# Attention over short sequences: the division of the outputs moves from VectorE to GpSimd, and the loads are issued five chunks ahead

## The chip, the cores and the metric

The kernel runs on one core of a Trainium2 chip. The metric is the device time of one execution in microseconds (us). Three runs of the kernel before took 143.09 us in the median (142.85 to 143.81). The profile is that of one further execution.

The core has five engines that run side by side and wait for one another through semaphores: TensorE (matmul, "PE" in the profile, its weight loads "PEld"), VectorE ("DVE"), ScalarE ("ACT"), GpSimd ("POOL") and SyncE ("SP"). Each works through its own list of instructions in order. Data come from HBM to SBUF and go back through 16 DMA engines. Matmuls write into PSUM, which has eight banks of 2 KB per partition. GpSimd issues the loads here, and SyncE the stores.

## The reference

```python
# q, k, v: (32, 12, 128, 64) float32: batch, heads, sequence, head dimension
scale = 1.0 / np.sqrt(64)
scores = scale * np.matmul(q, k.transpose(0, 1, 3, 2))
scores_max = np.max(scores, axis=-1, keepdims=True)
attn = np.exp(scores - scores_max)
attn = attn / (np.sum(attn, axis=-1, keepdims=True) + 1e-8)
return np.matmul(attn, v)
```

There are 384 heads of 128 x 64. Each input and the output hold 12.6 MB. The kernel leaves out the maximum (the inputs are small), and divides at the end: it multiplies the unnormalized outputs by the reciprocals of the row sums.

## The kernel before

The 384 heads are cut into NCH = 24 chunks of 16 heads. A chunk's q, k and v are three loads of 128 partitions x 1024 elements, which the DMA casts from float32 to bfloat16 on the way. Each partition holds runs of consecutive rows of one head (16 rows of q and k, 4 rows of v).

What happens to chunk c:

- `turn(c, 0)` and `turn(c, 1)`: VectorE transposes q and k in 32 x 32 blocks, SBUF to SBUF (tiles qt and kt), so that the head dimension comes to lie on the partitions.
- `scores(c)`: 32 small matmuls write all 16 score blocks to s_ps, which fills four PSUM banks and has one buffer; ScalarE takes the exponential of all 2048 columns in one instruction (attn).
- `values(c, part)`: two halves of v go through matmuls with a permuted identity (perm) into v_ps, one bank, and ScalarE copies them to v2 in SBUF.
- `denominators(c)`: four matmuls with a matrix of ones give the row sums (d_ps).
- `outputs(c, j)`: 16 matmuls for each half j of the head dimension give the transposed outputs (o_ps). d_ps and o_ps share a ring named w_ps.
- `divide(c, d_ps)`: VectorE turns the sums into SBUF (dt) and takes their reciprocals (recip, 16 per partition).
- `finish(c, j, o_ps)`: VectorE turns half j of the outputs, and multiplies it by the reciprocals into o_sb.
- `store(c)`: SyncE issues one DMA of 512 KB from o_sb.

The order of the instructions on each engine is the order of the Python code: everything stands under a manual schedule, and nothing reorders it. The body of the loop over c works on several chunks at once: scores of c+1, values of c+2, the turns of c+2, and denominators, outputs and store of c. On TensorE the order within one pass is scores(c+1), first half of values(c+2), denominators(c), outputs(c, 0), second half of values(c+2), outputs(c, 1).

Waits come from data and from buffers. A pool with `bufs` = n lets the writer of a tile wait for the readers of the tile n before it. Ahead of the loop GpSimd issues all 72 loads one behind the other. The input tiles of all 24 chunks have buffers of their own, so no load waits for a buffer; each load waits for the completion of the load eight places before it, whose semaphore it takes over. The stores wait for one another in the same way, eight places back.

PSUM's eight banks: s_ps four, v_ps one, w_ps two, ot_ps one. The last of these holds the turned outputs between the two steps of `finish`.

Of the kernel before, what the change touches and what calls it, by code (L numbers as in the profile page):

```python
# [9 lines left out]
@with_exitstack  # L10
def kernel(
    ctx: ExitStack,
    tc: tile.TileContext,
    q: bass.AP,
    k: bass.AP,
    v: bass.AP,
    out: bass.AP,
):

    nc = tc.nc
    f32 = mybir.dt.float32
    bf16 = mybir.dt.bfloat16

    B, H, S, D = q.shape
    assert S == 128 and D == 64
    scale = 1.0 / (D ** 0.5)
    TQ = 16  # L30
    GQ = S // TQ
    T = 4
    A = 4
    G = S // T
    CB = 4
    NCH = B * H // (A * CB)

    def runs(x, t):
        return x.rearrange("b h (g t) d -> (b h g) (t d)", t=t).rearrange(
            "(n p) x -> p n x", p=128)  # L40

    qr, kr, vr, orr = runs(q, TQ), runs(k, TQ), runs(v, T), runs(out, TQ)

    singles = ctx.enter_context(tc.tile_pool(name="singles", bufs=1))
    pin = ctx.enter_context(tc.tile_pool(name="pin", bufs=NCH))
    pt = ctx.enter_context(tc.tile_pool(name="pt", bufs=3))
    pa = ctx.enter_context(tc.tile_pool(name="pa", bufs=3))
    pf = ctx.enter_context(tc.tile_pool(name="pf", bufs=2))
    po = ctx.enter_context(tc.tile_pool(name="po", bufs=3))
    ps = ctx.enter_context(tc.tile_pool(name="ps", bufs=1, space=bass.MemoryType.PSUM))  # L50

    chunks, qts, attns, v2s, osbs = {}, {}, {}, {}, {}

    def load_qk(c):
        for src, which in ((qr, 0), (kr, 1)):
            x = pin.tile([128, TQ, D], bf16, tag="qk"[which] + "_bf", name="qk"[which] + "_bf")
            nc.gpsimd.dma_start(out=x, in_=src[:, c, :].rearrange("p (t d) -> p t d", t=TQ))  # L57
            chunks[c, which] = x

    def load_v(c):  # L60
        x = pin.tile([128, CB, T, D], bf16, tag="v_bf", name="v_bf")
        nc.gpsimd.dma_start(  # L62
            out=x, in_=vr[:, c * CB:(c + 1) * CB, :].rearrange("p n (t d) -> p n t d", t=T))
        chunks[c, 2] = x

    with tc.manual_schedule():
        load_qk(0)
        ident = singles.tile([128, 128], bf16)
        make_identity(nc, ident)
        perm = singles.tile([128, A, 4, GQ], bf16)  # L70
        nc.vector.tensor_copy(  # L71
            perm.rearrange("p a th g -> p a g th"),
            ident.rearrange("p (a g th) -> p a g th", a=A, th=4))
        ones = singles.tile([128, 32], bf16)
        nc.vector.memset(ones, 1.0)

        load_v(0)
        for c in range(1, NCH):
            if c < NCH - 1:
                load_v(c)  # L80
            load_qk(c)
        load_v(NCH - 1)

        def turn(c, which):


            x = chunks.pop((c, which)).bitcast(f32)
            xt = pt.tile([128, 4, S], f32, tag="qk"[which] + "t", name="qk"[which] + "t")
            if which == 0:
                nc.vector.transpose(xt.rearrange("p h (x g) -> p x h g", g=GQ), x)  # L90
            else:
                nc.vector.transpose(xt.rearrange("p h (x g) -> p x h g", g=GQ),  # L92
                                    x.rearrange("p (th tp) e -> p tp th e", tp=4))
            qts[c, which] = xt.bitcast(bf16).rearrange("p h (s j) -> p h s j", j=2)

        def scores(c):
            qt, kt = qts.pop((c, 0)), qts.pop((c, 1))
            s_ps = ps.tile([128, 4, 4, S], f32, tag="s_ps", name="s_ps")
            for h in range(4):
                for j in range(2):  # L100
                    for b in range(4):
                        pr = slice(b * 32, (b + 1) * 32)
                        nc.tensor.matmul(  # L103
                            s_ps[:, b, h, :], lhsT=kt[pr, h, :, j], rhs=qt[pr, h, :, j],
                            start=(j == 0), stop=(j == 1), tile_position=(b * 32, 0))
            attn = pa.tile([128, 4, 4, S], bf16, tag="attn", name="attn")
            nc.scalar.activation(out=attn, in_=s_ps, func=mybir.ActivationFunctionType.Exp,  # L107
                                 bias=0.0, scale=scale)
            attns[c] = attn

        def values(c, part):

            v_bf = chunks[c, 2]
            if part == 0:
                v2s[c] = pa.tile([128, A, CB, D], bf16, tag="v2", name="v2")
            v_ps = ps.tile([128, 2, CB, D], f32, tag="v_ps", name="v_ps")
            for i in range(2):
                for t in range(T):
                    nc.tensor.matmul(  # L119
                        v_ps[t * G:(t + 1) * G, i],  # L120
                        lhsT=perm[:, 2 * part + i].rearrange("p th g -> p (th g)"),
                        rhs=v_bf[:, :, t, :], start=True, stop=True, tile_position=(0, t * G))
            nc.scalar.copy(v2s[c][:, 2 * part:2 * part + 2], v_ps)  # L123

        def denominators(c):

            d_ps = ps.tile([128, 4, S], f32, tag="w_ps", bufs=2, name="d_ps")
            for b in range(4):
                nc.tensor.matmul(  # L129
                    d_ps[b * 32:(b + 1) * 32], lhsT=ones, rhs=attns[c][:, b],  # L130
                    start=True, stop=True, tile_position=(0, b * 32))
            return d_ps

        def outputs(c, j):

            o_ps = ps.tile([128, 4, S], f32, tag="w_ps", bufs=2, name="o_ps")
            for h in range(4):
                for b in range(4):
                    nc.tensor.matmul(  # L139
                        o_ps[b * 32:(b + 1) * 32, h], lhsT=v2s[c][:, h, b, j * 32:(j + 1) * 32],  # L140
                        rhs=attns[c][:, b, h], start=True, stop=True, tile_position=(0, b * 32))
            return o_ps

        def turned(src):
            return src.rearrange("p h (x g) -> p x h g", g=GQ)

        def divide(c, d_ps):
            dt = pf.tile([128, TQ, 32], f32, tag="dt", name="dt")
            nc.vector.transpose(dt, turned(d_ps))  # L149
            recip = pf.tile([128, TQ], f32, tag="recip", name="recip")  # L150
            nc.vector.reciprocal(recip, dt[:, :, 0])  # L151
            osbs[c] = (po.tile([128, TQ, D], f32, tag="o_sb", name="o_sb"), recip)

        def finish(c, j, o_ps):
            o_sb, recip = osbs[c]
            ot_ps = ps.tile([128, TQ, 32], f32, tag="ot_ps", name="ot_ps")
            nc.vector.transpose(ot_ps, turned(o_ps))  # L157
            nc.vector.tensor_mul(o_sb[:, :, j * 32:(j + 1) * 32], ot_ps,  # L158
                                 recip.to_broadcast([128, TQ, 32]))

        def store(c):
            o_sb, _ = osbs.pop(c)
            nc.sync.dma_start(out=orr[:, c, :], in_=o_sb.rearrange("p t d -> p (t d)"))

        e = NCH - 1
        for c in range(2):
            turn(c, 0)
            turn(c, 1)
        scores(0)
        values(0, 0)  # L170
        values(0, 1)
        for c in range(NCH):
            if c < e:
                scores(c + 1)
            if c == 0:
                values(1, 0)
                values(1, 1)
            if c + 2 < e:
                values(c + 2, 0)
            d_ps = denominators(c)  # L180
            o_ps0 = outputs(c, 0)
            if c + 2 < e:
                values(c + 2, 1)
            if c + 2 <= e:
                turn(c + 2, 0)
            divide(c, d_ps)
            o_ps1 = outputs(c, 1)
            if c + 1 == e:
                values(e, 0)
                values(e, 1)  # L190
            finish(c, 0, o_ps0)
            if c + 2 <= e:
                turn(c + 2, 1)
            finish(c, 1, o_ps1)
            store(c)


# [28 lines left out]
```

## Time and profile before

| | |
|---|---|
| median of three runs | 143.09 us |
| profiled execution | 143.61 us, of which the span of the trace is 141.8 us |
| granted TensorE clock | 1.00 throughout |
| VectorE busy | 116.4 us, 82% of the span |
| TensorE busy | 84.6 us, 60% |
| ScalarE busy | 72.1 us, 51% |
| GpSimd busy, all but a little of it issuing loads | 44.2 us, 31% |
| bytes | 37.75 MB read from HBM, 12.58 MB written to it |

How the rows are read. A row of groups gives the line of the kernel, the engine, the operation, what it writes and reads with shapes, how often, and behind the bars the busy time in us, the mean duration in ns, and the idle time of the engine just before, with what ended it. Row 2 of the page cuts the span into 40 slices of 3.5 us and gives the busy share in tenths; the row "DMA" is the mean over the 16 DMA engines. A DMA share above 1 in the windows means that the times of packets on one engine overlap. In a timeline the first number is the start and the second the duration; in brackets stands how long the engine was idle before and who released it. A row of SP in a timeline covers several issues, from the first to the last.

### The profile page before, as it was taken

Reading aid. Unit: us, or ns where it says so; the run is one execution under the profiler, and the core shown is the slowest. Engines: PE = TensorE matmul, PEld = TensorE weight load, DVE = VectorE, ACT = ScalarE, POOL = GpSimd, SP = SyncE. Lnnn points to the kernel's source line nnn. Section 1 sums busy time; section 2 is a strip of 40 time slices with the busy share of each in tenths; the row PEclk is TensorE's granted clock in tenths of the full one; section 3 lists DMA queues with packets and bytes.
Section 4 is the critical chain, followed back from the end, with each engine's and each line's share of the span. In section 5 each row is a group of like instructions: output and inputs, shape, how many; then the busy total and the mean of one; then the engine's idle time right before and its main releaser. Section 6 shows DMA issues by size and latency. Waiting matters only on the chain.

```text
span 141.8 us, 4551 instructions
## 1 busy us (share of the span) xinstructions
PE 84.6 (60%) x2016; PEld 57.6 (41%) x2016; DVE 116.4 (82%) x194; ACT 72.1 (51%) x73; POOL 44.2 (31%) x78
## 2 busy tenths in 40 slices
PE   0042476577666756856866675685685667575710
PEld 0031244444444534644544453464454445343400
DVE  1404249999999999999999999999999999998990
ACT  3061643465375366456547537645654753753500
POOL 6945535423233243252253133135132300000000
DMA  2999999999999999999999999999999999940333
GB/s 40 175 179 204 204 204 204 249 234 274 264 217 278 268 229 258 280 235 248 272 255 227 277 267 225 269 273 233 250 276 246 237 279 267 222 179 25 132 148 148
DMA packets 23059, 31.74 MB, mean 224 GB/s; under 512 B 1536, under 2 KB 13824, under 8 KB 23040
## 3 DMA queue, kind: packets, MB, share of 16 engines
q0 software_dynamic: 19584, 18.88, 81.0%
q1 hardware_dynamic: 3456, 12.58, 23.2%
q8 instruction: 15, 0.25, 0.7%
q14 instruction: 4, 0.03, 0.1%
HBM read 37.75 MB, written 12.58 MB: 355 GB/s over the span
## 4 chain that ended last, share of the span: by engine, by line
DVE 50%; PE 32%; DMA 6%; issue 5%; POOL 3%; ACT 2%; DVEq 0%; POOLq 0%
PE s_ps L103 16%; DVE ot_ps L157 13%; DVE o_sb L158 13%; DVE dt L149 12%; DVE kt L92 10%; PE v_ps L119 9%; PE d_ps L129 7%; DMA k_bf<-in_k_dram 6%; ACT attn L107 1%; DVE recip L151 1%; POOL v_bf L62 1%; ACT v L123 1%; POOL q_bf L57 1%; DVE qt L90 0%; POOL k_bf L57 0%
## 5 line engine op out<-in xcount | busy, mean ns | idle before, releaser
L107 ACT ACTIVATE attn<-s_ps 128x2048 bf16<-128x2048 f32 x24 | 45.0, 1877 | 43.2 <-PE s_ps L103 43.2
L119 PE MATMUL v_ps<-v_bf,perm 128*32 128x256 bf16 x384 | 29.7, 406 | 27.2 <-ACT v L123 27.0
L103 PE MATMUL s_ps<-qt,kt 32*128 32x128 bf16 x768 | 25.0, 301 | 22.6 <-DVE kt L92 22.6
L123 ACT CAST v<-v_ps 128x512 bf16<-128x512 f32 x48 | 28.0, 583 | 18.4 <-PE v_ps L119 18.4
L158 DVE TENSOR_TENSOR o_sb<-ot_ps,recip 128x512 f32<-128x512 f32 x48 | 33.2, 692 | 1.6
L157 DVE STREAM_TRANSPOSE ot_ps<-o_ps 128x512 f32<-128x512 f32 x48 | 33.2, 692 | 0.2
L139 PE MATMUL o_ps<-attn,v 128*32 128x128 bf16 x768 | 31.4, 312 | 1.4 <-DVE dt L149 1.3
L139 PEld LDWEIGHTS <-v 128*32 128x32 bf16 x768 | 26.0, 147 | 11.2 <-issue 8.4
L103 PEld LDWEIGHTS <-kt 32*128 32x128 bf16 x768 | 18.6, 131 | 28.9 <-DVE kt L92 28.9
L62 POOL DMA_DIRECT2D v_bf<-in_v_dram x24 | 18.1, 756 | 27.3 <-DMA q_bf<-in_q_dram 23.6
L119 PEld LDWEIGHTS <-perm 128*32 128x32 bf16 x384 | 10.6, 110 | 36.3 <-issue 36.2
L90 DVE STREAM_TRANSPOSE qt<-q_bf 128x512 f32<-128x512 f32 x24 | 16.9, 703 | 8.1 <-DMA q_bf<-in_q_dram 8.1
L149 DVE STREAM_TRANSPOSE dt<-d_ps 128x512 f32<-128x512 f32 x24 | 17.2, 715 | 7.0 <-PE d_ps L129 7.0
L57 POOL DMA_DIRECT2D k_bf<-in_k_dram x24 | 12.8, 533 | 24.0 <-DMA v_bf<-in_v_dram 22.8
L57 POOL DMA_DIRECT2D q_bf<-in_q_dram x24 | 12.9, 538 | 17.2 <-DMA k_bf<-in_k_dram 15.3
L92 DVE STREAM_TRANSPOSE kt<-k_bf 128x512 f32<-128x512 f32 x24 | 16.9, 703 | 1.1 <-DMA k_bf<-in_k_dram 1.1
L129 PE MATMUL d_ps<-attn,ones 128*32 128x512 bf16 x96 | 15.4, 631 | 0.0
L151 DVE RECIPROCAL recip<-dt 128x16 f32<-128x16 f32 x24 | 6.1, 253 | 0.8
L129 PEld LDWEIGHTS <-ones 128*32 128x32 bf16 x96 | 3.7, 145 | 1.5 <-issue 0.4
L71 DVE COPY perm<-ident 128x128 bf16<-128x128 bf16 x1 | 0.4, 447 | 3.0 <-POOL ident masks.py:199 3.0
L107 ACT ACT_TABLE_LOAD x1 | 1.3, 1283 | 0.7 <-PEq L210 0.7
masks.py:199 POOL TENSOR_SCALAR_AFFINE_SELECT ident<-ident 128x128 bf16<-128x128 bf16 x1 | 0.3, 287 | 0.1
(6 smaller groups left out, 0.7 us busy)
## 6 DMA issues: line engine op xcount, KB each, us to landing
out_dram<-o_sb SPq DMA_DIRECT2D x24, 512.0 KB, 6.6
q_bf<-in_q_dram POOLq DMA_DIRECT2D x24, 256.0 KB, 13.7
k_bf<-in_k_dram POOLq DMA_DIRECT2D x24, 256.0 KB, 13.8
v_bf<-in_v_dram POOLq DMA_DIRECT2D x24, 256.0 KB, 13.3
```

The source lines that it names most:

```text
L57: nc.gpsimd.dma_start(out=x, in_=src[:, c, :].rearrange("p (t d) -> p t d", t=TQ))
L62: nc.gpsimd.dma_start(out=x, in_=vr[:, c * CB:(c + 1) * CB, :].rearrange("p n (t d) -> p n t d", t=T))
L92: nc.vector.transpose(xt.rearrange("p h (x g) -> p x h g", g=GQ), x.rearrange("p (th tp) e -> p tp th e", tp=4))
L103: nc.tensor.matmul(s_ps[:, b, h, :], lhsT=kt[pr, h, :, j], rhs=qt[pr, h, :, j], start=(j == 0), stop=(j == 1), tile_position=(b * 32, 0))
L107: nc.scalar.activation(out=attn, in_=s_ps, func=mybir.ActivationFunctionType.Exp, bias=0.0, scale=scale)
L119: nc.tensor.matmul(v_ps[t * G:(t + 1) * G, i], lhsT=perm[:, 2 * part + i].rearrange("p th g -> p (th g)"), rhs=v_bf[:, :, t, :], start=Tru ...
L123: nc.scalar.copy(v2s[c][:, 2 * part:2 * part + 2], v_ps)
L129: nc.tensor.matmul(d_ps[b * 32:(b + 1) * 32], lhsT=ones, rhs=attns[c][:, b], start=True, stop=True, tile_position=(0, b * 32))
L139: nc.tensor.matmul(o_ps[b * 32:(b + 1) * 32, h], lhsT=v2s[c][:, h, b, j * 32:(j + 1) * 32], rhs=attns[c][:, b, h], start=True, stop=True, ...
L149: nc.vector.transpose(dt, turned(d_ps))
L157: nc.vector.transpose(ot_ps, turned(o_ps))
L158: nc.vector.tensor_mul(o_sb[:, :, j * 32:(j + 1) * 32], ot_ps, recip.to_broadcast([128, TQ, 32]))
```

## The change

Four things are done at once.

1. `finish` now only turns: VectorE writes the turned half straight from PSUM into o_sb. The tile ot_ps is gone, and its bank goes to the ring w_ps, which has three banks.
2. A new step `scale_rows(c)` multiplies the whole of o_sb (1024 elements per partition) by the reciprocals in place, on GpSimd, SBUF to SBUF. In the last chunk GpSimd takes one half and VectorE the other.
3. The loads of the first five chunks are issued ahead of the loop. The loads of chunk c+5 are issued in pass c, after the turns of the outputs and ahead of `scale_rows(c)`.
4. The input tiles have 11 buffers instead of 24. LAG is 0, so the store of c still follows in pass c, now behind GpSimd's multiply.

```diff
+    AHEAD = 5
+    LAG = 0
...
-    pin = ctx.enter_context(tc.tile_pool(name="pin", bufs=NCH))
+    pin = ctx.enter_context(tc.tile_pool(name="pin", bufs=AHEAD + 6))
...
-    po = ctx.enter_context(tc.tile_pool(name="po", bufs=3))
+    po = ctx.enter_context(tc.tile_pool(name="po", bufs=LAG + 3))
...
-        load_v(0)
-        for c in range(1, NCH):
+        def load(c):
             if c < NCH - 1:
                 load_v(c)
             load_qk(c)
-        load_v(NCH - 1)
+            if c == NCH - 1:
+                load_v(c)
+
+        load_v(0)
+        for c in range(1, AHEAD):
+            load(c)
...
-            d_ps = ps.tile([128, 4, S], f32, tag="w_ps", bufs=2, name="d_ps")
+            d_ps = ps.tile([128, 4, S], f32, tag="w_ps", bufs=3, name="d_ps")
...
-            o_ps = ps.tile([128, 4, S], f32, tag="w_ps", bufs=2, name="o_ps")
+            o_ps = ps.tile([128, 4, S], f32, tag="w_ps", bufs=3, name="o_ps")
...
         def finish(c, j, o_ps):
+            o_sb, _ = osbs[c]
+            nc.vector.transpose(o_sb[:, :, j * 32:(j + 1) * 32], turned(o_ps))
+
+        def scale_rows(c):
             o_sb, recip = osbs[c]
-            ot_ps = ps.tile([128, TQ, 32], f32, tag="ot_ps", name="ot_ps")
-            nc.vector.transpose(ot_ps, turned(o_ps))
-            nc.vector.tensor_mul(o_sb[:, :, j * 32:(j + 1) * 32], ot_ps,
-                                 recip.to_broadcast([128, TQ, 32]))
+            if c < NCH - 1:
+                nc.gpsimd.tensor_mul(o_sb, o_sb, recip.to_broadcast([128, TQ, D]))
+            else:
+                for eng, sl in ((nc.gpsimd, slice(0, 32)), (nc.vector, slice(32, 64))):
+                    eng.tensor_mul(o_sb[:, :, sl], o_sb[:, :, sl],
+                                   recip.to_broadcast([128, TQ, 32]))
...
             finish(c, 1, o_ps1)
+            if c + AHEAD < NCH:
+                load(c + AHEAD)
+            scale_rows(c)
+            if c >= LAG:
+                store(c - LAG)
+        for c in range(NCH - LAG, NCH):
             store(c)
```

What this does to the order on the engines is shown at three places. The lines of the changed kernel are numbered a little higher, since code was added.

VectorE, one pass of the loop in the kernel before (pass 1, which turns q and k of chunk 3 and finishes chunk 1; qt and kt are the turned inputs, dt the turned sums, ot_ps the turned outputs):

```order
L90 STREAM_TRANSPOSE qt<-q_bf 128x16x4x8
L149 STREAM_TRANSPOSE dt<-d_ps 128x512
L151 RECIPROCAL recip<-dt 128x16
L157 STREAM_TRANSPOSE ot_ps<-o_ps 128x512
L158 TENSOR_TENSOR o_sb<-ot_ps,recip 128x16x32
L92 STREAM_TRANSPOSE kt<-k_bf 128x16x4x8
L157 STREAM_TRANSPOSE ot_ps<-o_ps 128x512
L158 TENSOR_TENSOR o_sb<-ot_ps,recip 128x16x32
```

The same pass on VectorE in the changed kernel:

```order
L96 STREAM_TRANSPOSE qt<-q_bf 128x16x4x8
L155 STREAM_TRANSPOSE dt<-d_ps 128x512
L157 RECIPROCAL recip<-dt 128x16
L162 STREAM_TRANSPOSE o_sb<-o_ps 128x16x32
L98 STREAM_TRANSPOSE kt<-k_bf 128x16x4x8
L162 STREAM_TRANSPOSE o_sb<-o_ps 128x16x32
```

The two multiplies have left the pass, and the two turns of the outputs write o_sb; the order of the rest is as it was.

GpSimd, the loads of chunks 5 and 6 in the kernel before (v, q, k of chunk 5, then of chunk 6):

```order
L62 DMA v_bf<-in_v_dram 128x4x256
L57 DMA q_bf<-in_q_dram 128x1024
L57 DMA k_bf<-in_k_dram 128x1024
L62 DMA v_bf<-in_v_dram 128x4x256
L57 DMA q_bf<-in_q_dram 128x1024
L57 DMA k_bf<-in_k_dram 128x1024
```

The same loads on GpSimd in the changed kernel, with the multiplies of chunks 0 and 1:

```order
L64 DMA v_bf<-in_v_dram 128x4x256
L59 DMA q_bf<-in_q_dram 128x1024
L59 DMA k_bf<-in_k_dram 128x1024
L167 TENSOR_TENSOR o_sb<-o_sb,recip 128x1024
L64 DMA v_bf<-in_v_dram 128x4x256
L59 DMA q_bf<-in_q_dram 128x1024
L59 DMA k_bf<-in_k_dram 128x1024
L167 TENSOR_TENSOR o_sb<-o_sb,recip 128x1024
```

Between the loads of two chunks there is now a multiply, which waits for VectorE; from chunk 6 on, every load is queued behind the multiply of the chunk six before it.

GpSimd, the end of the program in the changed kernel (the last three loads are those of chunk 23; before the change the loads were the end):

```order
L167 TENSOR_TENSOR o_sb<-o_sb,recip 128x1024
L59 DMA q_bf<-in_q_dram 128x1024
L59 DMA k_bf<-in_k_dram 128x1024
L64 DMA v_bf<-in_v_dram 128x4x256
L167 TENSOR_TENSOR o_sb<-o_sb,recip 128x1024 x5
L170 TENSOR_TENSOR o_sb<-o_sb,recip 128x16x32
```

Behind the last load GpSimd has five whole multiplies (chunks 18 to 22) and the half of chunk 23.

## The prediction

> **What bounds the kernel now.** I read the page first, then the groups, the windows, the waits, and the instructions of one chunk in order of time. The page's first parts:
>
> ```profile
> span 141.8 us, 4551 instructions
> ...
> PE 84.6 (60%) x2016; PEld 57.6 (41%) x2016; DVE 116.4 (82%) x194; ACT 72.1 (51%) x73; POOL 44.2 (31%) x78
> DMA  2999999999999999999999999999999999940333
> q0 software_dynamic: 19584, 18.88, 81.0%
> q1 hardware_dynamic: 3456, 12.58, 23.2%
> HBM read 37.75 MB, written 12.58 MB: 355 GB/s over the span
> out_dram<-o_sb SPq DMA_DIRECT2D x24, 512.0 KB, 6.6
> q_bf<-in_q_dram POOLq DMA_DIRECT2D x24, 256.0 KB, 13.7
> ```
>
> VectorE looks like the bound with 82%. But the DMA row stands at 9 from the second slice to the 35th, so the 16 DMA engines have no free time either until about 124 us. What they deliver shows in the windows; the last two columns are the DMA share and the GB/s written (loads write bf16, half of the bytes that they read: 18.88 MB against 37.75 MB).
>
> ```profile
> 0.00:10.00 10.00, 1.66 (x40) 1.17 (x41) 1.88 (x4) 3.16 (x3) 7.61 (x17) 1.00 0.87 127
> 10.00:20.00 10.00, 4.37 (x92) 2.65 (x92) 2.58 (x4) 4.59 (x7) 4.14 (x7) 1.00 1.23 203
> 20.00:120.00 100.00, 68.08 (x1652) 47.00 (x1644) 94.77 (x159) 56.46 (x58) 32.49 (x54) 1.00 1.18 252
> 120.00:125.00 5.00, 3.40 (x89) 2.40 (x84) 4.73 (x9) 2.94 (x3) 0.00 (x0) 1.00 0.83 215
> ```
>
> From 10 to 20 us only loads run: 203 GB/s written is 406 GB/s read, and a load of 0.262 MB takes 1.29 us. From 20 to 120 us the core writes 25.2 MB. The rows of one chunk, and of the first store:
>
> ```profile
> 23.87 5.41 SPq L163 DMA_DIRECT2D out_dram<-o_sb  x2
> 68.28 1.04 PE L103 MATMUL s_ps<-qt,kt 32*128 32x128 bf16 x32 [0.48 <-DVE kt L92]
> 69.42 1.88 ACT L107 ACTIVATE attn<-s_ps 128x2048 bf16<-128x2048 f32 x1 [1.42 <-PE s_ps L103]
> 71.20 0.58 ACT L123 CAST v<-v_ps 128x512 bf16<-128x512 f32 x1
> 71.83 0.62 PE L119 MATMUL v_ps<-v_bf,perm 128*32 128x256 bf16 x8 [1.11 <-ACT v L123]
> 72.21 0.66 PE L139 MATMUL o_ps<-attn,v 128*32 128x128 bf16 x16
> 72.60 0.70 DVE L92 STREAM_TRANSPOSE kt<-k_bf 128x512 f32<-128x512 f32 x1
> 73.36 1.04 PE L103 MATMUL s_ps<-qt,kt 32*128 32x128 bf16 x32 [0.48 <-DVE kt L92]
> ```
>
> A chunk takes 73.36 − 68.28 = 5.08 us. So from the first store at 23.87 us to 120 us there are 96.1/5.08 = 18.9 stores of 0.524 MB, 9.9 MB. The other 15.3 MB are 58.4 loads, at 1.29 us 75.3 us; the 24.7 us left make 1.31 us per store. **DMA per chunk: 3 × 1.29 + 1.31 = 5.18 us**, as long as the chunk itself. Two bounds lie on one another.
>
> The third is the round of TensorE and ScalarE in these rows: scores, exp, first copy, second half of values, second half of outputs, next scores. TensorE waits only 0.48 us in it for VectorE, so without VectorE it takes 5.08 − 0.48 = 4.60 us.
>
> **VectorE, per chunk.** The groups:
>
> ```profile
> L158 DVE TENSOR_TENSOR o_sb<-ot_ps,recip 128x512 f32<-128x512 f32 x48 | 33.2, 692 | 1.6
> L157 DVE STREAM_TRANSPOSE ot_ps<-o_ps 128x512 f32<-128x512 f32 x48 | 33.2, 692 | 0.2
> L149 DVE STREAM_TRANSPOSE dt<-d_ps 128x512 f32<-128x512 f32 x24 | 17.2, 715 | 7.0 <-PE d_ps L129 7.0
> L90 DVE STREAM_TRANSPOSE qt<-q_bf 128x512 f32<-128x512 f32 x24 | 16.9, 703 | 8.1 <-DMA q_bf<-in_q_dram 8.1
> ```
>
> Two multiplies of 692 ns go: 1.38 us per chunk, 47 of 48 in all. The two turns stay, with another destination; the PSUM-to-SBUF turn of the same size took 715 ns, so they may cost 0.05 us per chunk more. VectorE's chunk falls from 5.08 to about 3.75 us, below both other bounds. What is late next is the 4.60 us round at first, then the DMA's 5.18 us. Only the gap between loads that ran ahead and a compute that lags is to be won.
>
> **GpSimd.** It takes 23 multiplies of 1024 elements and one of 512. No such instruction is in the trace. The nearest rows:
>
> ```profile
> masks.py:199 POOL TENSOR_SCALAR_AFFINE_SELECT ident<-ident 128x128 bf16<-128x128 bf16 x1 | 0.3, 287 | 0.1
> masks.py:197 POOL MEMSET ident<- 128x128 bf16 x1 | 0.2, 231 | 0.0
> L62 POOL DMA_DIRECT2D v_bf<-in_v_dram x24 | 18.1, 756 | 27.3 <-DMA q_bf<-in_q_dram 23.6
> L57 POOL DMA_DIRECT2D q_bf<-in_q_dram x24 | 12.9, 538 | 17.2 <-DMA k_bf<-in_k_dram 15.3
> ```
>
> By the memset's 231 ns for 128 elements, were a good half of it fixed, 1024 cost 1.1 us; by the select's 287/128 = 2.24 ns, 2.3 us; with two inputs read one after the other, twice that, 4.6 us. I take 2.3 us: the select also reads and writes SBUF. The Trainium skill speaks against the change here: "GPSIMD Engine Reference", section "Performance versus the Vector engine", calls GpSimd the wrong place for elementwise work and gives 4497 ns for a 2048-element two-input add against 2293 ns on VectorE. An estimate from it, half for half the elements, is 2.25 us, and the sum would be the same; no row here shows it.
>
> POOL then has 0.76 + 2 × 0.54 + 2.3 = 4.1 us per chunk, with semaphores some 4.3 us, under 5.18. Below nothing this cannot come: POOL does nothing less than before.
>
> **The loads behind the multiply.** GpSimd works in order, so the load of chunk c+6 is queued behind the multiply of c, which waits for VectorE's last turn of c, and SP's store waits for that multiply. Today a load is issued when the load eight places before it has landed (POOL waits for loads only; 13.7 us from issue to landing over 5.08/3 = 1.7 us per load is eight in flight). The start:
>
> ```profile
> 18.33 0.53 POOL L57 DMA_DIRECT2D k_bf<-in_k_dram  x1 [0.77 <-DMA v_bf<-in_v_dram]
> 20.29 0.75 POOL L62 DMA_DIRECT2D v_bf<-in_v_dram  x1 [1.43 <-DMA q_bf<-in_q_dram]
> 21.80 0.70 DVE L92 STREAM_TRANSPOSE kt<-k_bf 128x512 f32<-128x512 f32 x1
> 27.71 0.75 POOL L62 DMA_DIRECT2D v_bf<-in_v_dram  x1 [0.70 <-DMA q_bf<-in_q_dram]
> ```
>
> The first row is k of chunk 5, the last load ahead of the first multiply; the second is v of chunk 6. In the changed kernel kt (21.80 today, one multiply of 0.69 us earlier) and the last turn of chunk 0 end at about 22.6 us, the multiply at 24.9, and v of chunk 6 goes out 4.6 us later than today. The row at 27.71 is v of chunk 8, released by q of chunk 5: eight loads out at 18.9 us are landing until 28 us. So some three loads, 3.9 us of work, and the first store stand before the DMA when v of chunk 6 is issued. I take 0.3 us of gap, with bounds of 0 and 1.5 us. Later each multiply holds the next v back by about a microsecond (2.9 us of multiply and issue against 1.7 us between landings), while five to eight loads are out. I price that at nothing as long as the engines stay full; rival 2 prices it otherwise.
>
> **When the last k lands.** Written by 120 us: 1.27 + 2.03 + 25.2 = 28.5 MB. Less 9.9 MB of stores and 0.3 MB of other queues, 18.3 of 18.88 MB of loads: a good two are left, and k of chunk 23, the last but one, lands at about 122.5 us, with 19.3 stores done. VectorE turns it at 128.18 us, 5.7 us late:
>
> ```profile
> 112.33 0.75 POOL L62 DMA_DIRECT2D v_bf<-in_v_dram  x1 [1.55 <-DMA v_bf<-in_v_dram]
> 128.18 0.70 DVE L92 STREAM_TRANSPOSE kt<-k_bf 128x512 f32<-128x512 f32 x1
> 131.35 0.62 PE L139 MATMUL o_ps<-attn,v 128*32 128x128 bf16 x16 [0.40 <-DVE dt L149]
> 132.45 0.59 ACT L123 CAST v<-v_ps 128x512 bf16<-128x512 f32 x1 [0.48 <-PE v_ps L119]
> 133.79 0.69 DVE L158 TENSOR_TENSOR o_sb<-ot_ps,recip 128x512 f32<-128x512 f32 x1
> 134.40 0.71 DVE L149 STREAM_TRANSPOSE dt<-d_ps 128x512 f32<-128x512 f32 x1
> 137.60 0.69 DVE L158 TENSOR_TENSOR o_sb<-ot_ps,recip 128x512 f32<-128x512 f32 x1
> ```
>
> In the changed kernel compute keeps up, so more stores go before that k: store 20 is half done, 20.4 in all. That is 1.1 × 1.31 = 1.4 us more, and with the gap k lands at 122.5 + 1.4 + 0.3 = **124.2 us**. Compute could be there at 21.1 + 21 × 4.60 = 117.7 us, so the DMA sets it.
>
> **The tail.** From this turn to the end of the span it is 141.8 − 128.18 = 13.6 us today. With three banks the second outputs of chunk 22 no longer wait for dt (0.40 us), the copy at 132.45 comes 0.48 us earlier, and dt at 134.40, which stood behind the multiply at 133.79, 0.7 us earlier: 133.7. Then dt 0.72, reciprocal 0.25, two turns 0.72 each, half a multiply 0.69 and issue: 137.0 us if GpSimd's half (2.3/2 = 1.15 us, started after the first turn) lies beside it, 137.7 if they run in succession. The store needs 141.8 − 138.29 = 3.5 us as now. The tail is 12.3 to 13.0 us; I take 12.5.
>
> **Sum.** 124.2 + 12.5 = 136.7 us of span, against 141.8. The profiled execution took 143.61 us, 1.8 us beside its span: 138.5 us; it lies 0.5 us above the median of 143.09, so 138.0 us, 3.6% faster. Bounds of the terms: gap 0 to 1.5, tail −0.2 to +0.5, stores ±0.5, landing ±1: 136 to 140.
>
> **Rivals.**
> 1. The round decides: transfers get quicker as soon as they are asked for sooner. Then 117.7 + 12.5 + 1.8 − 0.5 = 131.5 us. Against it: 406 GB/s of traffic in the load-only window and (25.2 + 15.3)/100 us = 405 GB/s with stores, a constant rate, DMA share above 1 in both. 0.09.
> 2. The rate depends on how many loads are out. The multiply holds v back 1.2 us and q and k some 0.2 us, 0.5 us on the mean of 13.7 us from issue to landing: 4%, 0.2 us per chunk over 19 chunks, 3.8 us: 141.8 us, no measurable change. For it: the end, where the eight last loads drain, is weaker (215 GB/s). 0.12.
> 3. The bytes are capped at the mean of 355 GB/s: 50.33 MB need 141.8 us again, 143 us. The windows' 405 GB/s speak against it. The Trainium skill, "DMA: Bandwidth & Descriptors", section "Bandwidth", lets about 358 GB/s of HBM bind such transfers, which gives 140.6 us for the bytes alone; the 406 GB/s here contradict that for one busy core. 0.04.
> 4. Slower: the GpSimd multiply is dear and POOL becomes the bound, since loads and stores stand behind it. It leaves the shadow at 5.18 − 2.0 = 3.2 us and eats the 5 us of gain at 3.4 us (19 chunks × 0.26). At the upper bound of 4.6 us a round is 6.6 us: 22.6 + 19 × 6.6 + 4 × 4.6 + 2.3 + 3.5 + 1.8 = 174 us. 0.10.
>
> The forecast keeps 0.65.
>
> **The numbers.** One per cent, 1.4 us, is about what a measurement here can tell from none. Faster by more: the forecast and rival 1, 0.74. Within: rivals 2 and 3, 0.16. Slower: rival 4, 0.10. The range takes in the forecast's 136 to 140, rival 2 above, and half of the way to rival 1 below: 133.5 to 142.0.
>
> **What would show it.** VectorE's busy time near 84 us (116.4 − 32.5), with idle time ended by the loads of q and k in the last third; the windows from 30 to 110 us at about 250 GB/s or more and DMA share near 1.18; GpSimd's multiply at 2.3 us; the turn of the last k near 124 us, straight after its landing. Wrong: a DMA share under 1.1 in the middle (rival 2), a POOL that waits for no load (rival 4), or VectorE's turns waiting for stores of three chunks before.

## The result

The changed kernel took 137.94 us in the median of four runs (137.68 to 138.44), the kernel before 143.2 us (142.85 to 143.81). The ratio is 0.963, with a 95% interval of 0.959 to 0.968: 3.7% faster. The profiled execution took 138.44 us, with a span of 136.5 us. A run that lies more than 1.5% above the fastest run of the same kernel counts as slow, and the ratios here and below leave it out.

The page of the changed kernel, the rows that answer to those shown of before:

```profile
span 136.5 us, 4560 instructions
...
PE 79.2 (58%) x2016; PEld 54.2 (40%) x2016; DVE 83.9 (61%) x147; ACT 72.1 (53%) x73; POOL 89.5 (66%) x102
...
DMA  2999999999999999999999999999999999997333
...
HBM read 37.75 MB, written 12.58 MB: 369 GB/s over the span
```

VectorE has lost 32.5 us of work and the span only 5.3 us. The DMA row stands at 9 up to slice 36, which ends at 36 × 3.41 = 122.9 us; before, it did so up to slice 35, which ended at 35 × 3.55 = 124.1 us. So the DMA is full for about as long as before. The groups say what each engine does now, and what ended its waits:

```profile
L167 POOL TENSOR_TENSOR o_sb<-o_sb,recip 128x1024 f32<-128x1024 f32 x23 | 43.9, 1909 | 14.9 <-DVE o_sb L162 10.7
L96 DVE STREAM_TRANSPOSE qt<-q_bf 128x512 f32<-128x512 f32 x24 | 16.9, 703 | 30.6 <-DMA q_bf<-in_q_dram 30.6
L162 DVE STREAM_TRANSPOSE o_sb<-o_ps 128x512 f32<-128x512 f32 x48 | 32.0, 669 | 1.5 <-PE o_ps L145 1.3
L170 POOL TENSOR_TENSOR o_sb<-o_sb,recip 128x512 f32<-128x512 f32 x1 | 1.0, 1047 | 0.5 <-POOL o_sb L167 0.5
```

The turn of q waited 8.1 us for its load before; now it waits 30.6 us. That is where most of VectorE's free time went. The windows (the last two columns are the DMA share and the GB/s written):

```profile
20.00:110.00 90.00, 59.06 (x1535) 40.77 (x1524) 62.43 (x111) 53.38 (x55) 65.86 (x70) 0.66 1.19 253
110.00:120.00 10.00, 5.88 (x152) 4.08 (x156) 6.57 (x13) 5.53 (x6) 5.10 (x4) 0.59 1.16 252
120.00:125.00 5.00, 3.26 (x99) 2.24 (x93) 4.51 (x9) 2.46 (x2) 1.90 (x1) 0.50 0.96 251
125.00:136.50 11.50, 4.86 (x120) 3.23 (x120) 5.82 (x10) 2.94 (x3) 4.85 (x3) 0.50 0.41 167
```

From 20 to 110 us the DMA writes 253 GB/s at a share of 1.19, against 252 and 1.18 from 20 to 120 us before. The transfers have not become faster, and they have not got further either: by 122.5 us the DMA has written 29.3 MB in either kernel (236 GB/s over the first 110 us, 256 over the next 10 and 294 over the last 2.5 before; 237, 252 and 268 now). One pass in order of time, VectorE:

```profile
70.52 0.71 DVE L96 STREAM_TRANSPOSE qt<-q_bf 128x512 f32<-128x512 f32 x1 [1.38 <-DMA q_bf<-in_q_dram]
71.16 0.67 DVE L155 STREAM_TRANSPOSE dt<-d_ps 128x512 f32<-128x512 f32 x1
71.93 0.25 DVE L157 RECIPROCAL recip<-dt 128x16 f32<-128x16 f32 x1
72.10 0.65 DVE L162 STREAM_TRANSPOSE o_sb<-o_ps 128x512 f32<-128x512 f32 x1
72.99 0.71 DVE L98 STREAM_TRANSPOSE kt<-k_bf 128x512 f32<-128x512 f32 x1 [0.23 <-DMA k_bf<-in_k_dram]
73.63 0.68 DVE L162 STREAM_TRANSPOSE o_sb<-o_ps 128x512 f32<-128x512 f32 x1
75.68 0.71 DVE L96 STREAM_TRANSPOSE qt<-q_bf 128x512 f32<-128x512 f32 x1 [1.38 <-DMA q_bf<-in_q_dram]
```

The pass is 75.68 − 70.52 = 5.16 us, and VectorE stands idle at its head until q lands. The end of the program:

```profile
121.86 0.71 DVE L96 STREAM_TRANSPOSE qt<-q_bf 128x512 f32<-128x512 f32 x1 [0.34 <-DMA q_bf<-in_q_dram]
124.19 0.66 DVE L98 STREAM_TRANSPOSE kt<-k_bf 128x512 f32<-128x512 f32 x1
131.33 1.05 POOL L170 TENSOR_TENSOR o_sb<-o_sb,recip 128x512 f32<-128x512 f32 x1 [0.52 <-POOL o_sb L167]
131.82 1.10 DVE L170 TENSOR_TENSOR o_sb<-o_sb,recip 128x512 f32<-128x512 f32 x1
```

The last turn of k starts at 124.19 us, and from there it is 12.3 us to the end. Where the 5.3 us come from is seen when the landing of this k is set beside its turn. Its issue, first in the kernel before, then in the changed one:

```profile
110.26 0.53 POOL L57 DMA_DIRECT2D k_bf<-in_k_dram  x1 [1.23 <-DMA k_bf<-in_k_dram]
110.47 0.53 POOL L59 DMA_DIRECT2D k_bf<-in_k_dram  x1 [0.74 <-DMA k_bf<-in_k_dram]
```

In both traces it lands 13.3 us after its issue: at 123.6 us before and at 123.8 us now. Before, VectorE turned it at 128.18 us, 4.6 us after the landing; now it turns it 0.4 us after. These 4.2 us are most of the gain. The rest is the tail, 13.6 us before and 12.3 us now, and the landing, 0.2 us later, takes a little back.

### The profile page after: what moved, and what is told of

It is laid out like the page before. It is cut to its first block, busy times and chain, and to the rows that moved or that the text cites. A ratio compares the mean times of both kernels' runs of the same rounds, so it can differ in the third digit from the quotient of the medians.

```text
span 136.5 us, 4560 instructions
## 1 busy us (share of the span) xinstructions
PE 79.2 (58%) x2016; PEld 54.2 (40%) x2016; DVE 83.9 (61%) x147; ACT 72.1 (53%) x73; POOL 89.5 (66%) x102
## 4 chain that ended last, share of the span: by engine, by line
DMA 46%; issue 13%; POOL 13%; PE 10%; DVE 9%; ACT 6%; POOLq 0%; DVEq 0%; ACTq 0%
DMA k_bf<-in_k_dram 36%; DMA q_bf<-in_q_dram 9%; PE s_ps L109 5%; ACT attn L113 4%; POOL o_sb L167 3%; POOL q_bf L59 3%; POOL v_bf L64 3%; PE v_ps L125 3%; DVE o_sb L162 3%; DVE dt L155 3%; ACT v L129 2%; DVE kt L98 2%; POOL k_bf L59 2%; PE d_ps L135 1%; DVE o_sb L170 1%
## 5 line engine op out<-in xcount | busy, mean ns | idle before, releaser
L167 POOL TENSOR_TENSOR o_sb<-o_sb,recip 128x1024 f32<-128x1024 f32 x23 | 43.9, 1909 | 14.9 <-DVE o_sb L162 10.7
L125 PE MATMUL v_ps<-v_bf,perm 128*32 128x256 bf16 x384 | 28.8, 386 | 27.7 <-ACT v L129 25.7
L109 PE MATMUL s_ps<-qt,kt 32*128 32x128 bf16 x768 | 22.9, 283 | 23.6 <-DVE kt L98 23.6
L96 DVE STREAM_TRANSPOSE qt<-q_bf 128x512 f32<-128x512 f32 x24 | 16.9, 703 | 30.6 <-DMA q_bf<-in_q_dram 30.6
L162 DVE STREAM_TRANSPOSE o_sb<-o_ps 128x512 f32<-128x512 f32 x48 | 32.0, 669 | 1.5 <-PE o_ps L145 1.3
L145 PE MATMUL o_ps<-attn,v 128*32 128x128 bf16 x768 | 29.4, 299 | 0.0
L109 PEld LDWEIGHTS <-kt 32*128 32x128 bf16 x768 | 17.1, 123 | 29.2 <-DVE kt L98 29.0
L145 PEld LDWEIGHTS <-v 128*32 128x32 bf16 x768 | 25.0, 140 | 8.1 <-issue 5.3
L59 POOL DMA_DIRECT2D k_bf<-in_k_dram x24 | 12.9, 538 | 17.9 <-DMA v_bf<-in_v_dram 15.7
L155 DVE STREAM_TRANSPOSE dt<-d_ps 128x512 f32<-128x512 f32 x24 | 16.6, 690 | 8.2 <-PE d_ps L135 8.0
L64 POOL DMA_DIRECT2D v_bf<-in_v_dram x24 | 19.3, 804 | 3.1 <-DMA q_bf<-in_q_dram 1.5
L170 POOL TENSOR_TENSOR o_sb<-o_sb,recip 128x512 f32<-128x512 f32 x1 | 1.0, 1047 | 0.5 <-POOL o_sb L167 0.5
## 6 DMA issues: line engine op xcount, KB each, us to landing
q_bf<-in_q_dram POOLq DMA_DIRECT2D x24, 256.0 KB, 12.7
k_bf<-in_k_dram POOLq DMA_DIRECT2D x24, 256.0 KB, 13.3
v_bf<-in_v_dram POOLq DMA_DIRECT2D x24, 256.0 KB, 12.7
```

The source lines that it names most:

```text
L64: nc.gpsimd.dma_start(out=x, in_=vr[:, c * CB:(c + 1) * CB, :].rearrange("p n (t d) -> p n t d", t=T))
L109: nc.tensor.matmul(s_ps[:, b, h, :], lhsT=kt[pr, h, :, j], rhs=qt[pr, h, :, j], start=(j == 0), stop=(j == 1), tile_position=(b * 32, 0))
L125: nc.tensor.matmul(v_ps[t * G:(t + 1) * G, i], lhsT=perm[:, 2 * part + i].rearrange("p th g -> p (th g)"), rhs=v_bf[:, :, t, :], start=Tru ...
L145: nc.tensor.matmul(o_ps[b * 32:(b + 1) * 32, h], lhsT=v2s[c][:, h, b, j * 32:(j + 1) * 32], rhs=attns[c][:, b, h], start=True, stop=True, ...
L162: nc.vector.transpose(o_sb[:, :, j * 32:(j + 1) * 32], turned(o_ps))
L167: nc.gpsimd.tensor_mul(o_sb, o_sb, recip.to_broadcast([128, TQ, D]))
```

## The experiments

Ratios are to the kernel before on the same chip, where its median lay between 143.2 and 143.9 us.

**Was the DMA the bound before, and is it now?** The same eleven stores are left out of either kernel.

```diff
-            store(c)
+            if c % 2 == 0 or c == e:
+                store(c)
```

> The kernel before, without the stores of the odd chunks 1 to 21 (11 of 24 stores left out; those chunks' outputs are not written). Theory: before the change VectorE's 5.08 us per chunk set the end, and the transfers ran beside it with a price of 1.31 us per store that nobody waited for: 143 us, at most 1 us less. Rival: the DMA engines already set the end before the change: 11 x 1.31 = 14 us less, 129 us.

Measured: 143.48 us, ratio 1.002 (0.998 to 1.005). The windows of this run:

```profile
20.00:110.00 90.00, 59.42 (x1508) 41.09 (x1504) 85.73 (x144) 50.87 (x54) 32.47 (x54) 0.70 1.20 228
110.00:120.00 10.00, 6.81 (x172) 4.73 (x168) 9.46 (x17) 5.75 (x6) 0.00 (x0) 0.50 0.18 61
```

From 110 us on the DMA is nearly idle (share 0.18), VectorE is as busy as ever (9.46 of 10 us), and the span is 141.8 us as before. In the kernel before, the bytes of these stores cost nothing, although the DMA row was full.

> The changed kernel without the same 11 stores. Theory: after the change the DMA's 5.18 us per chunk set the end; with 3 x 1.29 + 0.6 = 4.5 us they no longer do, and the round of TensorE and ScalarE takes over, which ran at 4.47 us in the first passes (scores at 21.64, 26.11 and 30.58 us): last k turned at 20.9 + 21 x 4.47 = 114.8 us, plus the tail of 12.3 and 1.9 beside the span: 129 us. Rival: the chain VectorE, GpSimd, SyncE sets the pace of 5.15 us, whatever is transferred: 138 us.

Measured: 127.54 us, ratio 0.888 (0.882 to 0.893). With fewer bytes the changed kernel gains some 10 us where the kernel before gained nothing. Its passes take some 4.4 us, and the last k is turned at 113.2 us. The chain from VectorE over GpSimd to SyncE does not set the pace of 5.16 us; the transfers do. What sets the 4.4 us is not separated: from 60 to 100 us the DMA share is still 1.21, and the turn of q still waits 14.7 us in all for its loads, so the transfers and the round of TensorE and ScalarE lie close together.

**Did the multiply have to go to GpSimd?**

```diff
-                nc.gpsimd.tensor_mul(o_sb, o_sb, recip.to_broadcast([128, TQ, D]))
+                nc.vector.tensor_mul(o_sb, o_sb, recip.to_broadcast([128, TQ, D]))
```

> The changed kernel, but with VectorE doing the whole multiply of 1024 elements out of SBUF in chunks 0 to 22. Theory: VectorE has 5.08 - 1.38 + 1.2 = 4.9 us per chunk, still under the DMA's 5.18, so the steady stage is as in the changed kernel and only the tail, where VectorE stands in the way, grows by 1 to 2 us: 139 to 140 us. Rival: the gain comes from the multiply having left VectorE, and goes with its return: 142 to 143 us.

Measured: 140.6 us, ratio 0.981 (0.975 to 0.987), 0.6 us above the upper end of the theory's range and under the rival's. About half of the gain stays with the multiply on VectorE, whose busy time is 109.4 us instead of 116.4. One instruction of 1024 elements (1.23 us) is cheaper than two of 512 (1.38 us), and the turns are a little shorter. The window from 20 to 110 us is again at 253 GB/s. The loss is at the end: the last k lands at 123.6 us, as in the kernel before, and is turned at 125.81 us, behind a VectorE that has not waited since 119.20 us. It is 2.2 us late, where the kernel before was 4.6 us late and the changed kernel is 0.4. The loads five chunks ahead were not tried alone in the kernel before; since the last k lands at the same time in all three, they did not bring it in sooner.

**What does GpSimd's multiply cost?** A further multiply into an unused tile stands ahead of each, once over half of the elements, once over all.

```diff
+                spare = pf.tile([128, TQ, 32], f32, tag="spare", name="spare")
+                nc.gpsimd.tensor_mul(spare, o_sb[:, :, 0:32], recip.to_broadcast([128, TQ, 32]))
                 nc.gpsimd.tensor_mul(o_sb, o_sb, recip.to_broadcast([128, TQ, D]))
```

> The changed kernel with a further multiply of 512 elements into an unused tile on GpSimd ahead of each multiply (1.05 us more per chunk). Theory: 1.91 + 1.05 + 1.88 of issuing = 4.8 us per chunk lie under 5.18 us of DMA, nothing waits: 138 to 139 us. Rival: GpSimd is on the path, since loads and stores stand behind its multiply, and every microsecond counts: 23 x 1.05 = 24 us more, 162 us.

Measured: 138.12 us, ratio 0.965 (0.956 to 0.973). GpSimd is busy for 84.0 of the 90 us from 20 to 110 us, and the kernel is as fast as with 65.9.

> The changed kernel with a further multiply of all 1024 elements into an unused tile on GpSimd ahead of each multiply. Theory (a threshold at 5.18 us per chunk): 2 x 1.91 + 1.88 of issuing and some gaps = 5.8 to 5.9 us per chunk, now over the DMA's 5.18, so GpSimd sets the pace over 19 chunks, 12 to 14 us more, and the last multiplies and the stores behind them add a few more: 150 to 157 us. Rival (there is slack elsewhere, loads are so far ahead that GpSimd never decides): 138 to 140 us.

Measured: 152.44 us, ratio 1.058 (1.051 to 1.065). GpSimd in order of time:

```profile
62.59 1.94 POOL L168 TENSOR_TENSOR spare<-o_sb,recip 128x1024 f32<-128x1024 f32 x1
64.61 1.90 POOL L169 TENSOR_TENSOR o_sb<-o_sb,recip 128x1024 f32<-128x1024 f32 x1
66.45 0.82 POOL L64 DMA_DIRECT2D v_bf<-in_v_dram  x1
67.26 0.54 POOL L59 DMA_DIRECT2D q_bf<-in_q_dram  x1
67.78 0.55 POOL L59 DMA_DIRECT2D k_bf<-in_k_dram  x1
68.33 1.94 POOL L168 TENSOR_TENSOR spare<-o_sb,recip 128x1024 f32<-128x1024 f32 x1
```

No idle time stands in brackets: the pass is 68.33 − 62.59 = 5.74 us of GpSimd alone. So 1 us more costs nothing and 1.9 us cost 14 us: a threshold. It lies between GpSimd's passes in the two runs, 4.9 us (65.22 − 60.34, also without idle time) and 5.74 us, where the DMA's pass of 5.16 us would put it.

**How far ahead must the loads be?**

```diff
-    AHEAD = 5
+    AHEAD = 3
```

> The changed kernel with loads three chunks ahead instead of five (and 9 input buffers instead of 11). Theory: the rate of the DMA engines does not depend on how many loads are out as long as they have work; with one chunk and a half of loads in flight this just holds, and the loop multiply, issue, landing, turn over two chunks comes to 10.3 to 11 us, 5.2 to 5.5 per chunk: 139 to 146 us. Rival (rate in proportion to the loads in flight, 4 to 5 instead of 7 to 8): 7 us or more per chunk, over 170 us.

Measured: 172.28 us, ratio 1.196 (1.184 to 1.208). Both expectations missed: the theory by 26 us, and the rival gave the time but not for its reason. From the multiply at 42.04 us to the one fourteen passes later at 134.29 us a pass takes 6.6 us. A load lands 6.5 us (v) to 7.5 us (q and k) after its issue in the median, so some three are in flight, instead of seven to eight; a rate in proportion would have made the passes about twice as long as 5.16 us. VectorE and GpSimd in this run, from two timelines:

```profile
71.49 0.54 POOL L59 DMA_DIRECT2D q_bf<-in_q_dram  x1
75.04 1.90 POOL L167 TENSOR_TENSOR o_sb<-o_sb,recip 128x1024 f32<-128x1024 f32 x1 [2.47 <-issue]
78.17 0.71 DVE L96 STREAM_TRANSPOSE qt<-q_bf 128x512 f32<-128x512 f32 x1 [3.27 <-DMA q_bf<-in_q_dram]
81.73 1.90 POOL L167 TENSOR_TENSOR o_sb<-o_sb,recip 128x1024 f32<-128x1024 f32 x1 [2.97 <-issue]
```

The multiply before these rows started at 68.83 us. Behind it q goes out at 71.49, lands and is turned at 78.17, and the multiply of that pass starts at 81.73. So the loop over two passes takes 81.73 − 68.83 = 12.9 us: 2.7 to the issue, 6.7 for the landing, 3.6 from the turn of q to the multiply. The expectation had 10.3 to 11 us for it. The DMA wrote 200 GB/s with a share of 1.05 in the middle. Whether a shallower queue alone lowers the rate was not separated from this loop.

> The changed kernel with loads eight chunks ahead instead of five (14 input buffers), stores as in the changed kernel. Theory formed on the run with later stores: the multiply of chunk c stands on GpSimd behind the loads of chunk c+8, the last of which waits until v of chunk c+6 has landed, so multiplies, and through the two buffers of reciprocals VectorE, are tied to loads far ahead; the loads are done early, but the compute lags and ends late: VectorE waits for GpSimd before reciprocals (15 us in the run with later stores), the last k is turned at 124 to 126 us although it landed by 120, and the time is 139 to 142 us. Rival (more loads ahead cannot harm, the loss in the run with later stores came from moving the stores to ScalarE): 138 us.

```diff
-    AHEAD = 5
+    AHEAD = 8
```

Measured: 144.63 us, ratio 1.007 (1.002 to 1.012): the whole gain is gone, and the time is 2.6 us above the upper end of the theory's range. The waits of the profiled execution, which with 145.71 us was the longest of ten (what waited, for what, us in total, how often, the longest):

```profile
DVE o_sb L162 <- DMA out_dram<-o_sb: 12.0, 10, 2.6
DVE recip L157 <- POOL o_sb L167: 5.0, 4, 4.1
```

Multiplies that stand behind far loads delay the reciprocals as expected (5.0 us instead of 15), but more than that the stores: with three output buffers the turn of the outputs waits for the store of three chunks before (12.0 us). Neither wait is in the changed kernel. In this execution the last k lands at 120.9 us, 2.9 us sooner than in the changed kernel, and is turned only at 132.44 us: the loads are early and the compute is late, as the theory had it, though by more. Farther ahead is not safer here, because the loads and the multiplies share one queue in order.

**Is the bank of any use?**

```diff
-tag="w_ps", bufs=3
+tag="w_ps", bufs=2
```

> The changed kernel with two banks in the ring of sums and outputs, as before the change (one bank stays unused). Theory: the wait of the second outputs for dt lies in the shadow of the DMA in the steady stage, and only the tail gets it back, 0.4 to 0.8 us: 138.3 to 138.8 us. Rival (the third bank carries the steady stage): 0.4 us per chunk, 147 us.

Measured: 139.69 us in the median of three runs (138.26 to 139.97; a fourth took 140.77), ratio 0.967 (0.960 to 0.974), which lies within the interval of the changed kernel. The rival's 147 us are excluded. From the last turn of k to the end it is 137.8 − 124.93 = 12.9 us, against 12.3 with three banks. That fits the 0.4 to 0.8 us expected in the tail, as far as one execution of each can show it; the rest of the distance is a last k that was turned 0.7 us later in this execution.

**Can stores make room for the last loads?** If the DMA is full until the last k has landed and half empty afterwards, stores should go last. On ScalarE's queue, behind its copies, a store keeps its place in the program.

```diff
-            nc.sync.dma_start(out=orr[:, c, :], in_=o_sb.rearrange("p t d -> p (t d)"))
+            nc.scalar.dma_start(out=orr[:, c, :], in_=o_sb.rearrange("p t d -> p (t d)"))
...
                 values(c + 2, 1)
+            if c > LAG:
+                store(c - LAG - 1)
...
-            if c >= LAG:
-                store(c - LAG)
-        for c in range(NCH - LAG, NCH):
+        for c in range(NCH - LAG - 1, NCH):
             store(c)
```

LAG, AHEAD and the numbers of buffers are given with each run.

> The changed kernel with every store issued three chunks later, from ScalarE's queue behind its copies (so that it really waits for its place in the program), with loads eight chunks ahead and seven output buffers. Theory: the order of transfers matters, since the DMA is full until the last k has landed and half empty after it (share 0.41 over 11.5 us): three stores of 1.31 us fewer stand before that k, so it lands 3.9 us earlier, and the three run in the tail beside the compute: 134 us (133.5 to 135). Rival: the bytes are the same, so is the time: 138 us.

Measured with LAG = 3, AHEAD = 8 and seven output buffers: 141.68 us, ratio 0.984 (0.979 to 0.989), slower than the changed kernel and outside both expectations. VectorE waited 15.1 us for GpSimd ahead of its reciprocals, and the last k was turned at 124.94 us though it had landed at 116.6 us. The eight chunks of lead, not the order of the stores, were to blame: the run with eight ahead alone was no faster.

> The changed kernel with every store two chunks later on ScalarE's queue, loads five chunks ahead as in the changed kernel, four buffers for the reciprocals and seven for the outputs, so that no multiply waits for far loads and no reciprocal for a multiply. Theory: two stores of 1.31 us fewer stand before the last k, it lands 2.6 us earlier, and the stores run in the half-empty tail: 135 to 136 us. Rival (the order of the same bytes does not matter): 138 us.

Measured with LAG = 2, AHEAD = 5, four buffers of reciprocals and seven of outputs: 138.1 us, ratio 0.958 (0.951 to 0.966). The 2.6 us were not won: the last k lands at 122.6 us, 1.2 us sooner than in the changed kernel, and is turned at 123.68 us, 0.5 us sooner. A window tells a part of why:

```profile
30.00:40.00 10.00, 5.66 (x248) 4.21 (x237) 9.05 (x17) 7.92 (x8) 9.52 (x11) 0.95 1.09 186
```

Without stores in the first passes the DMA has only loads to do, and five chunks ahead it runs short of them: share 1.09 and 186 GB/s, against 1.22 and 203 in the ten microseconds before. By the share that is about 1 us of the 2.1 that are missing at the turn; the rest was not traced to its cause.

> As the run with stores two chunks later, but with loads six chunks ahead, so that the loads can use the DMA time that the first stores leave free. Theory: five ahead leaves the DMA short of loads in the first passes without stores for up to 1 us, six does not, while the multiplies wait a little longer for loads, which the additional buffers absorb: 134.5 to 136 us. Rival (each chunk further ahead ties the multiplies to later loads, as with eight): 138 us or more.

Measured with LAG = 2, AHEAD = 6 and the same buffers for reciprocals and outputs: 135.6 us (135.3 to 136.36), ratio 0.943 (0.937 to 0.949). The same window has a share of 1.20, and the last k is turned at 121.59 us, 2.6 us ahead of the changed kernel, which is the price of two stores. When this k lands, 17 stores have landed, against 19 in the changed kernel. This version beats both kernels; against the changed kernel it was not run on one chip, but the intervals of the two ratios do not touch. Six chunks ahead with the stores left in their place was not run.

> As the run with stores two later and loads six ahead, with stores three later. Theory: one more store of 1.31 us leaves the stretch ahead of the last k, but the first passes have one more without a store, in which the loads come up against the limit of six chunks, so about half of it is won: 0.5 to 1 us less than the 135.6 us of that run, 134.6 to 135.1 us. Rival (the stores that are left for the tail now fill it and set the end): 135.6 us or more.

Measured with LAG = 3, AHEAD = 6 and eight buffers of outputs: 135.61 us, ratio 0.946 (0.943 to 0.949): nothing more. The last k is turned at 120.20 us, 1.4 us earlier still, but the last row of compute is this one:

```profile
127.84 1.10 DVE L170 TENSOR_TENSOR o_sb<-o_sb,recip 128x512 f32<-128x512 f32 x1
```

It ends at 128.94 us, and the span at 134.0: 5.1 us from there to the end, which is the last store, instead of 136.5 − 132.92 = 3.6 in the changed kernel and 133.8 − 129.91 = 3.9 with the stores two later. So the stores that were put off stand in the way of the last one, as the rival had it.

## Why the prediction was right

- **Three bounds on one another** (VectorE and the DMA at 5.08 and 5.18 us, the round of TensorE and ScalarE below): right. The pass settled at 5.16 us. Taking stores away gained nothing before, with VectorE busy as ever, and some 10 us after. The round showed itself where the DMA does not decide: scores started every 4.47 us in the first passes, a little under the predicted 4.60. It is not fixed, though: around 38 us two passes took 3.7 us each, and there the 32 matmuls of the scores took 0.64 us instead of 1.04. VectorE's waits for q began at 44.74 us, not in the last third, so compute caught up with the loads sooner than forecast.
- **GpSimd's multiply at 2.3 us**: too dear. It took 1.91 us; the upper bound of 4.6 was far off. Since it lies in the shadow, nothing followed from it. The estimate from the Trainium skill, "GPSIMD Engine Reference", section "Performance versus the Vector engine", 2.25 us, was 18% too high. The rule there that elementwise work is slower on GpSimd holds here (1.91 us against 1.23 on VectorE in the third experiment), and did not decide.
- **The threshold of rival 4**, 3.2 us per chunk for the multiply: borne out as far as two points can: 2.97 us cost nothing and 3.84 us made GpSimd the bound.
- **No gap at the start**: right. v of chunk 6 went out at 24.11 us (24.9 predicted), and the DMA share from 20 to 30 us is 1.23.
- **The last k at 124.2 us, straight after its landing**: the number was right in part by luck. The prediction let this k land at 122.5 us before the change, and 1.4 + 0.3 us later after it, for 1.1 more stores ahead of it and a gap. It landed at 123.6 us before, 1.1 us later than estimated, and at 123.8 us now, so of the 1.7 us only 0.2 came; by that landing 19 stores had landed in full in either kernel. Nor was it turned straight after: the row at 124.19 has no wait. VectorE had waited for q until 121.86, and then had the sums, the reciprocals and a turn to do ahead of k, which made 0.4 us. These misses of 1.1, −1.5 and 0.4 us cancel. What held is the mechanism: the transfers keep their rate, and what is won is the lag of compute behind the last landing, 5.7 us in the prediction and 4.6 us in the trace.
- **The tail**, 12.5 us: 12.3. The forecast took the two halves of the last multiply to lie beside one another, at 0.69 us for VectorE's. It took 1.10 us, while GpSimd's took 1.05, as much as a multiply of 512 elements took on it in the fourth experiment (1.07), so only VectorE's half was slower.
- **The sum**: 136.7 us of span against 136.5, with the misses above in it.
- **Rival 1**, transfers that get quicker, fell: 253 GB/s against 252. **Rival 2**, a rate that follows the number of loads in flight, did not show at five ahead (253 GB/s with seven or eight in flight, by 12.7 to 13.3 us from issue to landing and three loads in 5.16 us). At three ahead the rate was lower, with a loop that accounts for the time. **Rival 3** fell: the mean over the span is now 369 GB/s instead of 355.
- Named as a sign of error was also a turn that waits for the store of three chunks before. It did not occur at five ahead, and was the larger of the two waits at eight.

## What to carry to other kernels

When two resources take the same time per pass, relieving one gains only the lead that the other had built up: here 4.2 of 5.3 us, while 32.5 us of work went. Add up the bytes that are still to come before pricing the work that is removed. An instruction put on an engine that also issues transfers ties the two together in order: it can then be too close to its loads (a loop over the landing time) or too far behind them (buffers held up), and the right distance has to be counted in passes on both sides. When the transfers are the bound, put off what nobody waits for until the stretch in which they are half idle, and no further than that stretch holds.

## What the runs showed that was not expected

- The granted TensorE clock was 1.00 in the profiled run of the kernel before, 0.68 in that of the changed kernel, and 0.695 in the kernel before with fewer stores, whose span is nevertheless 141.8 us as before. The 32 matmuls of one chunk's scores took 1.04 us at a granted 1.00 and at 0.50, and 0.64 us in some short stretches (at 35.28 us in the changed kernel, at a granted 1.00). The clock row says nothing here of where the time went.
- One distance, chunks ahead, moved the time from 172 us (three) over 138 (five) to 145 (eight), more than the multiply itself ever cost.
- A VectorE multiply of 512 elements with both inputs in SBUF took 1.10 us while GpSimd multiplied, and 0.69 us before with one input in PSUM and GpSimd not multiplying. One of 1024 elements with both inputs in SBUF took 1.23 us in the third experiment, where GpSimd does not multiply beside it.
